# Dilated-attention transposes issued half a block later, MLP up products as one 512-column and one 256-column matmul

## The chip, the cores and the metric

One core of a Trainium2 chip runs the whole program. The metric is the device time of one launch in microseconds; the kernel before took 1325.72 us, the median of three runs (1324.39 to 1327.46).

## The reference, cut to what matters

Two transformer blocks run one after the other on 256 tokens of width 1024, in float32. The first block has four layers (Fourier mixing, grouped-query attention, dilated attention, Fourier mixing), each with a memory attention, a gate, an output projection and a layer norm. The second has two layers, each of three parallel mixers and a squared-ReLU MLP.

```
# first block, dilated layer (i = 2): three groups of 16 heads, rotated q and k, one softmax over the groups
for g, (window, dil) in enumerate(DIL_PAIRS):
    qg = apply_rope(qkv[:, :, 0, g], ang_1d)
    kg = apply_rope(qkv[:, :, 1, g], ang_1d)
    og, lg = dilated_group_attention(qg, kg, qkv[:, :, 2, g], dil, window // (2 * dil))
...
# second block, end of each of its two layers: h is 256 x 1024, w1 1024 x 4096, w2 4096 x 1024
jnp.square(jax.nn.relu(h @ w1)) @ w2
```

## The kernel before, in words

Every large product runs in three float32r matmuls: each operand is cut into a high part (a cast, on ScalarE) and a low part (the difference, on VectorE), and high by high, high by low and low by high are summed in one PSUM bank (class `Group`, `add`, line 221). The weights come in pieces of 128 x 1024 by DMA on SP's queue, are cut by `split_w` (lines 162 and 164) and used in the order of `plan()`. The activations are held transposed as `xTh` and `xTl`, [128, 8, 256] each: eight chunks of 128 features by 256 tokens. PSUM has eight banks, in four tags: `acc` (3), `sc` (2), `tp` (2), `pv` (1).

The framework puts each engine's instructions into one order, ahead of the run, by its own simulated timeline and by priority in program order; on the chip each engine then executes its list in that order. `tc.issue_after(ins)` forces instructions behind `ins` on its engine.

Dilated layer (`layer_dilated`): after one block for the memory queries, 18 blocks of 512 projected columns follow; `proj_N` computes a block in four steps of 12 matmuls (each step one weight piece for both halves of the tokens) into two `acc` banks, one for each half of 128 tokens. A block holds four 128-column kinds; a pair of heads has nine kinds (q and k of three groups, then three v), so that a q and its k can lie in two blocks. `rope` (line 714) rotates q and k: for each half, two VectorE products into the tiles `t1` and `t2` (lines 726, 727; two buffers each), and two GpSimd additions into `t1` (line 204). As soon as q and k of a group are both rotated, four TensorE transposes (line 899) put them into one `sc` bank, which is then cut into high and low. `weave` runs two steps of the blocks and then a step of each live pair of heads (`pair_dilated`: scores at line 238 into two `sc` banks, softmax at line 835 and after, transposes at line 537, values at lines 850 and 857). A pair becomes ready when its last v has been cut.

Between the dilated layer and the last Fourier layer the normed rows of x are transposed by `transpose_x` (line 306) with order "seq": four transposes into one `sc` bank, and then four casts and four differences of 128 x 128, each of which reads the bank in permuted column order (lines 193, 194). With the other orders it is one cast and one difference of 128 x 512.

MLP (end of `layer2`): 4096 hidden columns in eight blocks of 512. `up0` computes the first block; `up(b)` the seven others with `proj_T`: for each of four weight pieces, four chunks of 128 hidden columns and two chunks of features, three matmuls with 256 moving columns (the tokens), two chunks in one bank of two `tp` banks. A bank is then evacuated by a ReLU on ScalarE, a product on VectorE, a cast and a difference. `down(n, hf)` multiplies a hidden chunk by its row of w2, six matmuls of 512 columns for each half, into four banks (two `acc`, two `sc`) that stay open over the whole MLP. The order is up(b+1), then the eight calls of down for block b.

Of the kernel before, what the change touches and what calls it, by code (L numbers as in the profile page):

```python
# [17 lines left out]
P = 128  # L18
# [58 lines left out]
def kernel(ctx: ExitStack, tc: tile.TileContext, x_in, wall, vec, tabs, small, out, dbg=None):  # L77
# [113 lines left out]
    def split(h, l, src, scale=None, eng=None):  # L191
        if scale is None:
            A.copy(out=h, in_=src)  # L193
            return (eng or V).tensor_tensor(out=l, in0=src, in1=h.bitcast(F32), op=ALU.subtract).ins  # L194
        else:
            A.activation(out=h, in_=src, func=AF.Copy, scale=scale)
            return (eng or V).scalar_tensor_tensor(
                out=l, in0=src, scalar=scale, in1=h.bitcast(F32), op0=ALU.mult, op1=ALU.subtract).ins
# [49 lines left out]
    def hl(pair, f):  # L248
        return f(pair[0]), f(pair[1])
# [26 lines left out]
    mhalf = cst.tile([P, 12], F32, name="mhalf")  # L276
    G.memset(mhalf, -0.5)
    x = cst.tile([P, 2, D], F32, name="x")
    xTh = cst.tile([P, 8, T], F32R, name="xTh")
    xTl = cst.tile([P, 8, T], F32R, name="xTl")  # L280
    for n in range(4):
        load_raw(n)
    nc.sync.dma_start(x[:, 0, :], x_in[0:P, :])
# [17 lines left out]
    def transpose_x(hf, blk, src, order_):  # L301


        tp = scp([P, 4, P])
        for j in range(4):
            PE.transpose(tp[:, j, :], src[:, j * P:(j + 1) * P], ident)
        k = slice(4 * blk, 4 * blk + 4)
        if order_ == "seq":
            for j in range(4):
                f = lambda t: t[:, 4 * blk + j, hf * P:(hf + 1) * P].rearrange("p (a b c) -> p a b c", a=8, b=4, c=4)  # L310
                r = split(f(xTh), f(xTl), tp[:, j, :].rearrange("p (c b a) -> p a b c", a=8, b=4, c=4))
        else:
            c = slice(hf, T, 2) if order_ == "class" else slice(hf * P, (hf + 1) * P)
            r = split(xTh[:, k, c], xTl[:, k, c], tp)
        sc_read.append(r)

    def mm_out(dst, key, ys, npieces, by_class=False, ready=lambda i: True, n_end=0):
# [399 lines left out]

    def rope(ps, n, cos, sin, w, eng=None):

        t1 = ab.tile([P, 512], F32, tag="t1", name="t1", bufs=2)  # L720
        t2 = ab.tile([P, 512], F32, tag="t2", name="t2", bufs=2)
        v = lambda t: t[:, :n * 64].rearrange("p (n d) -> p n d", d=64)
        b = lambda t: t.unsqueeze(1).to_broadcast([P, n, 64])
        src = ps.rearrange("p (n d) -> p n d", d=64)
        with tc.high_priority():
            V.tensor_tensor(out=v(t1), in0=src, in1=b(cos), op=ALU.mult)
            V.tensor_tensor(out=v(t2), in0=src, in1=b(sin), op=ALU.mult)  # L727
        four = lambda t: t[:, :n * 64].rearrange("p (n t w) -> p n t w", t=2, w=w)
        for s in range(2):
            pool_add(four(t1)[:, :, s, :], four(t1)[:, :, s, :], four(t2)[:, :, 1 - s, :])  # L730
        return t1
# [130 lines left out]
    def layer_dilated(i):  # L862
        key = "c"
        kinds = []
        for p in range(8):
            kinds += [(p, "q", 0), (p, "k", 0), (p, "q", 1), (p, "k", 1), (p, "q", 2), (p, "k", 2)]
            kinds += [(p, "v", 0), (p, "v", 1), (p, "v", 2)]
        roped, vt, qm = {}, {}, []

        def projections(b):  # L870
            ps = yield from proj_N(key, 1 + b)
            cur = kinds[4 * b:4 * b + 4]
            s = 0
            while s < 4:
                e = s
                while e < 4 and (cur[e][1] == "v") == (cur[s][1] == "v") and cur[e][0] == cur[s][0]:
                    e += 1
                for hf in range(2):
                    src = ps[hf][:, s * P:e * P]
                    if cur[s][1] != "v":  # L880
                        r = rope(src, 2 * (e - s), rtab[:, hf, 2, :], rtab[:, hf, 3, :], 32)
                        for n in range(s, e):
                            roped[cur[n], hf] = r[:, (n - s) * P:(n - s + 1) * P]
                    else:
                        for n in range(s, e):
                            if cur[n] not in vt:
                                vt[cur[n]] = ph([P, 2, 2, P])
                            t = vt[cur[n]]
                            with tc.high_priority():
                                split(t[:, 0, hf, :], t[:, 1, hf, :], ps[hf][:, n * P:(n + 1) * P])  # L890
                s = e
            for p in range(8):
                for g in range(3):
                    kk = [(p, "q", g), (p, "k", g)]
                    if all((a, 0) in roped for a in kk):
                        tp = scp([P, 2, T])
                        for s, a in enumerate(kk):
                            for hf in range(2):
                                PE.transpose(tp[:, s, hf * P:(hf + 1) * P], roped.pop((a, hf)), ident)
                        t = (ph([P, 2, T]), ph([P, 2, T]))  # L900
                        sc_read.append(split(t[0], t[1], tp))
                        vt[p, "qk", g] = t

        def fill():
            qm.append((yield from tail(key, 0, True)))
            for b in range(18):
                yield from projections(b)
            yield from gates(key, 19)
            yield from out_and_norm(i, ORDER[2], "seq")

        def ready(c):
            return bool(qm) if c >= 8 else (c, "v", 2) in vt

        def pair(c):
            if c >= 8:
                return memory_pair(qm[0], c - 8)
            return pair_dilated([vt.pop((c, "qk", g)) for g in range(3)], [vt.pop((c, "v", g)) for g in range(3)], c)

        weave(fill(), [(lambda c=c: ready(c), lambda c=c: pair(c)) for c in ORDER[2]], 2, 3)

        for hf in range(2):
            for c in range(4):
                nc.gpsimd.dma_start(
                    scratch[hf * P:(hf + 1) * P, :].rearrange("(a b c) d -> c b a d", a=8, b=4, c=4)[c],
                    x[32 * c:32 * c + 32, hf, :])
        for hf in range(2):
            nc.gpsimd.dma_start(x[:, hf, :], scratch[hf * P:(hf + 1) * P, :])
# [88 lines left out]
    def layer2(l):  # L1016
# [371 lines left out]
                hid[k] = (hs[k // 2 * 2][:, k % 2, :], hs[k // 2 * 2 + 1][:, k % 2, :])  # L1388

        def up(b):  # L1390
            ps = run(proj_T(f"m1{l}", b, alloc=tpp))
            for j in range(2):
                s = pt([P, 2, T])
                A.activation(out=s, in_=ps[j], func=AF.Relu)
                V.tensor_tensor(out=s, in0=s, in1=ps[j], op=ALU.mult)
                h_, l_ = ph2([P, 2, T]), ph2([P, 2, T])
                split(h_, l_, s)
                for k in range(2):
                    hid[4 * b + 2 * j + k] = (h_[:, k, :], l_[:, k, :])
# [212 lines left out]
```

## Time and profile before

| what | value |
|---|---|
| median of three runs | 1325.72 us |
| time of the profiled execution | 1325.35 us |
| its span | 1323.6 us |
| TensorE busy | 1268.0 us (96%), 7550 matmuls |
| VectorE busy | 961.0 us (73%) |
| ScalarE busy | 750.6 us (57%) |
| GpSimd busy | 179.7 us (14%) |
| HBM traffic | 156 GB/s over the span |

The span is the time from the first to the last instruction of the profiled execution; its own time is 1.75 us longer. A busy share is an average over stages, and matmuls are pipelined: the duration of one is longer than the distance from its start to the start of the next, so what one costs is read from the starts.

### The profile page before, as it was taken

The page shows a single profiled execution, that of the slowest core. Times are in us where ns is not written, and L with a number is a line of the kernel's source. Part 1 is how long each engine was busy: PE and PEld are TensorE (multiplying, and loading weights), DVE is VectorE, ACT ScalarE, POOL GpSimd, SP SyncE. Part 2 cuts the span into 40 slices and gives each one's busy share as a digit, 9 for nine tenths or more (in the row PEclk, how much of TensorE's full clock was granted, in tenths as well). Part 3 has the DMA queues.
Part 4 walks back from the last instruction along what each step waited for, and adds up shares of the span by engine and source line. Part 5 has one row for each costly group of instructions (what it writes and reads, how often), then busy time and mean ns, then how long its engine had stood idle before and what let it go on. Part 6 is the DMA issues. An engine that isn't in the chain of part 4 may idle for free. (4 is left out here: it accounts for less than half of the span.)

```text
span 1323.6 us, 21769 instructions
## 1 busy us (share of the span) xinstructions
PE 1268.0 (96%) x7550; PEld 1090.7 (82%) x7550; DVE 961.0 (73%) x1950; ACT 750.6 (57%) x1673; POOL 179.7 (14%) x290
## 2 busy tenths in 40 slices
PE   8999998899999999998998999999999999999997
PEld 6987896688778878897986897899897897789896
DVE  7788887788778767777777896755556886665654
ACT  5664676555555645663653785545454774554543
POOL 1131500111112111122132201000001201000000
PEclk9999999999999999999998999999999999999999
DMA  8564542264334534355564543565664443366651
GB/s 289 175 221 144 163 148 80 92 194 158 108 121 153 158 115 128 128 169 174 177 198 138 184 138 110 178 205 181 186 187 151 145 154 127 132 218 185 184 189 49
DMA packets 64062, 209.53 MB, mean 158 GB/s; under 512 B 8520, under 2 KB 10192, under 8 KB 63952
## 3 DMA queue, kind: packets, MB, share of 16 engines
q1 hardware_dynamic: 60480, 203.33, 47.9%
q0 software_dynamic: 1888, 3.15, 0.8%
q10 hardware_dynamic: 1584, 1.67, 0.4%
q8 instruction: 59, 0.97, 0.3%
q14 instruction: 51, 0.42, 0.1%
HBM read 204.97 MB, written 2.10 MB: 156 GB/s over the span
## 5 line engine op out<-in xcount | busy, mean ns | idle before, releaser
L164 DVE TENSOR_TENSOR wl<-raw,wh 128x512 fp32r<-128x512 f32 (+3 forms) x756 | 502.7, 690 | 201.1 <-ACT wh L162 195.6
L162 ACT CAST wh<-raw 128x512 fp32r<-128x512 f32 (+3 forms) x756 | 441.8, 608 | 299.4 <-issue 74.7
L221 PE MATMUL acc<-wh,ph 128*128 128x512 f32 (+2 forms) x672 | 224.1, 389 | 6.3 <-ACT ph L548 2.0
L221 PE MATMUL acc<-wh,xTh 128*128 128x512 f32 (+3 forms) x560 | 218.7, 392 | 3.6 <-ACT xTh L193 2.2
L221 PE MATMUL acc<-wl,xTh 128*128 128x512 f32 (+3 forms) x560 | 216.9, 388 | 3.6 <-DVE wl L164 3.6
L221 PE MATMUL acc<-wh,xTl 128*128 128x512 f32 (+3 forms) x560 | 216.0, 388 | 2.5 <-DVE xTl L194 2.5
L221 PEld LDWEIGHTS acc<-wh,ph 128*128 128x128 f32 x672 | 125.1, 189 | 36.5 <-ACT ph L193 4.6
L221 PE MATMUL acc<-wl,ph 128*128 128x512 f32 (+2 forms) x336 | 130.3, 388 | 0.0
L221 PE MATMUL tp<-xTl,wh 128*128 128x256 f32 x448 | 126.6, 283 | 0.0
L221 PE MATMUL tp<-xTh,wl 128*128 128x256 f32 x448 | 126.6, 283 | 0.0
L221 PE MATMUL tp<-xTh,wh 128*128 128x256 f32 x448 | 126.6, 283 | 0.0
L221 PEld LDWEIGHTS acc<-wh,xTh 128*128 128x128 f32 x560 | 107.1, 191 | 23.5 <-ACT xTh L193 4.1
L221 PEld LDWEIGHTS acc<-wh,xTl 128*128 128x128 f32 x560 | 106.8, 191 | 23.1 <-DVE xTl L194 5.1
L221 PEld LDWEIGHTS acc<-wl,xTh 128*128 128x128 f32 x560 | 107.1, 191 | 21.6 <-DVE wl L164 4.3
L221 PE MATMUL sc<-wh,ph 128*128 128x512 f32 (+1 forms) x328 | 104.2, 369 | 0.0
L221 PE MATMUL acc<-xTh,wh 128*128 128x256 f32 x336 | 96.2, 287 | 0.0
L221 PE MATMUL acc<-xTh,wl 128*128 128x256 f32 x336 | 96.0, 286 | 0.0
L221 PE MATMUL acc<-xTl,wh 128*128 128x256 f32 x336 | 95.6, 285 | 0.0
L204 POOL TENSOR_TENSOR t<-t,t 128x256 f32<-128x256 f32 (+3 forms) x84 | 54.1, 673 | 268.4 <-DVE t L727 238.7
L221 PEld LDWEIGHTS tp<-xTl,wh 128*128 128x128 f32 x448 | 85.6, 191 | 0.5
L221 PEld LDWEIGHTS tp<-xTh,wh 128*128 128x128 f32 x448 | 85.5, 191 | 0.6
L221 PEld LDWEIGHTS tp<-xTh,wl 128*128 128x128 f32 x448 | 85.7, 191 | 0.0
(263 smaller groups left out, 2105.9 us busy)
## 6 DMA issues: line engine op xcount, KB each, us to landing
raw<-in_wall_dram SPq DMA_DIRECT2D x338, 512.0 KB, 3.9
raw<-in_wall_dram SPq DMA_DIRECT2D x20, 384.0 KB, 3.7
ph<-in_vec_dram SPq DMA_DIRECT2D x20, 256.0 KB, 6.0
raw<-in_wall_dram SPq DMA_DIRECT2D x8, 422.0 KB, 4.0
gn<-in_vec_dram SPq DMA_DIRECT2D x5, 512.0 KB, 4.7
raw<-in_wall_dram SPq DMA_DIRECT2D x6, 288.0 KB, 3.1
raw<-in_wall_dram SPq DMA_DIRECT2D x6, 256.0 KB, 3.9
x<-in_x_in_dram SPq DMA_DIRECT2D x2, 512.0 KB, 8.0
```

What stands on the lines that cost most here:

```text
L162: ih = A.copy(out=h[:, :k], in_=t[:, c]).ins
L164: il = V.tensor_tensor(out=l[:, :k], in0=t[:, c], in1=h[:, :k].bitcast(F32), op=ALU.subtract).ins
L204: G.tensor_tensor(out=out, in0=a, in1=b, op=ALU.add)
L221: done[0] = PE.matmul(out=self.out, lhsT=s, rhs=m, start=(i == 1), stop=(i == bk["n"]), skip_group_check=True).ins
```

## The change

Four edits:

1. `xTh` and `xTl` become the two halves of one tile `xT` [128, 8, 2, 256], so that a feature chunk's high and low part lie side by side.
2. For order "seq" the transposes write the permuted column order into PSUM, and one cast and one difference of 128 x 512 follow, as with the other orders.
3. In the dilated layer the transposes of a rotated group are not issued at the end of its block: the group is put on the list `waiting`, and `flush` issues the transposes after two of the four steps of the next block, behind the last matmul of a `Group`. After the last block it is called once more. The rotated tiles move from the tag `t1` (2 buffers) to a tag `rot` of 4 buffers, and a pair is ready when its three rotated groups are there as well as its last v.
4. `up(b)` multiplies the high weights by high and low activations in one matmul of 512 columns and the low weights by the high activations in one of 256, each chunk in a bank of its own (two `tp`, one `pv`, one `acc`). The evacuation copies the second half of the bank (ScalarE), adds the first (VectorE), and computes the squared ReLU in one VectorE instruction.

```diff
-    xTh = cst.tile([P, 8, T], F32R, name="xTh")
-    xTl = cst.tile([P, 8, T], F32R, name="xTl")
+    xT = cst.tile([P, 8, 2, T], F32R, name="xT")
+    xTh, xTl = xT[:, :, 0, :], xT[:, :, 1, :]
...
         for j in range(4):
-            PE.transpose(tp[:, j, :], src[:, j * P:(j + 1) * P], ident)
+            to = tp[:, j, :].rearrange("p (a b c) -> p c b a", a=8, b=4, c=4) if order_ == "seq" else tp[:, j, :]
+            PE.transpose(to, src[:, j * P:(j + 1) * P], ident)
         k = slice(4 * blk, 4 * blk + 4)
-        if order_ == "seq":
-            for j in range(4):
-                f = lambda t: t[:, 4 * blk + j, hf * P:(hf + 1) * P].rearrange("p (a b c) -> p a b c", a=8, b=4, c=4)
-                r = split(f(xTh), f(xTl), tp[:, j, :].rearrange("p (c b a) -> p a b c", a=8, b=4, c=4))
-        else:
-            c = slice(hf, T, 2) if order_ == "class" else slice(hf * P, (hf + 1) * P)
-            r = split(xTh[:, k, c], xTl[:, k, c], tp)
+        c = slice(hf, T, 2) if order_ == "class" else slice(hf * P, (hf + 1) * P)
+        r = split(xTh[:, k, c], xTl[:, k, c], tp)
...
-        t1 = ab.tile([P, 512], F32, tag="t1", name="t1", bufs=2)
+        t1 = pool1.tile([P, 512], F32, tag="rot", name="rot", bufs=4)
...
+        def flush():
+            with tc.issue_after(done[0]):
+                for p, g, rs in waiting:
+                    tp = scp([P, 2, T])
+                    for n, r in enumerate(rs):
+                        PE.transpose(tp[:, n // 2, (n % 2) * P:(n % 2 + 1) * P], r, ident)
+                    t = (ph([P, 2, T]), ph([P, 2, T]))
+                    sc_read.append(split(t[0], t[1], tp))
+                    vt[p, "qk", g] = t
+            waiting.clear()
+        def behind_half(steps):
...
+                n += 1
+                if n == 2:
+                    flush()
+                yield
         def projections(b):
-            ps = yield from proj_N(key, 1 + b)
+            ps = yield from behind_half(proj_N(key, 1 + b))
...
-                        tp = scp([P, 2, T])
-                        for s, a in enumerate(kk):
-                            for hf in range(2):
-                                PE.transpose(tp[:, s, hf * P:(hf + 1) * P], roped.pop((a, hf)), ident)
-                        t = (ph([P, 2, T]), ph([P, 2, T]))
-                        sc_read.append(split(t[0], t[1], tp))
-                        vt[p, "qk", g] = t
+                        waiting.append((p, g, [roped.pop((a, hf)) for a in kk for hf in range(2)]))
...
             for b in range(18):
                 yield from projections(b)
+            flush()
...
-            return bool(qm) if c >= 8 else (c, "v", 2) in vt
+            return bool(qm) if c >= 8 else all((c, *k) in vt for k in (("qk", 0), ("qk", 1), ("qk", 2), ("v", 2)))
...
         def up(b):
-            ps = run(proj_T(f"m1{l}", b, alloc=tpp))
+            ps = [f([P, 2, T]) for f in (tpp, tpp, pvp, acc)]
+            for i in range(4):
+                w = W(f"m1{l}", 4 * b + i)
+                for c in range(4):
+                    for kk in range(2):
+                        k = 2 * i + kk
+                        h_, l_ = hl(w, lambda t: t[:, kk * 512 + c * P:kk * 512 + (c + 1) * P])
+                        PE.matmul(out=ps[c], lhsT=h_, rhs=xT[:, k, :, :], start=(k == 0), stop=False, skip_group_check=True)
+                        done[0] = PE.matmul(out=ps[c][:, 0, :], lhsT=l_, rhs=xTh[:, k, :], start=False, stop=(k == 7),
+                                            skip_group_check=True).ins
             for j in range(2):
-                s = pt([P, 2, T])
-                A.activation(out=s, in_=ps[j], func=AF.Relu)
-                V.tensor_tensor(out=s, in0=s, in1=ps[j], op=ALU.mult)
+                r, s = pt([P, 2, T]), pt([P, 2, T])
+                for k in range(2):
+                    A.copy(out=r[:, k, :], in_=ps[2 * j + k][:, 1, :])
+                    V.tensor_tensor(out=s[:, k, :], in0=ps[2 * j + k][:, 0, :], in1=r[:, k, :], op=ALU.add)
+                V.scalar_tensor_tensor(out=s, in0=s, scalar=0.0, in1=s, op0=ALU.max, op1=ALU.mult)
                 h_, l_ = ph2([P, 2, T]), ph2([P, 2, T])
                 split(h_, l_, s)
```

## Rows read from the trace of the kernel before

**Rows 1.** The page's busy shares (busy us, share of the span, instructions).

```profile
PE 1268.0 (96%) x7550; PEld 1090.7 (82%) x7550; DVE 961.0 (73%) x1950; ACT 750.6 (57%) x1673; POOL 179.7 (14%) x290
```

**Rows 2.** Waits of TensorE: line, releaser, us in total, times, longest us.

```profile
PE sc L899 <- POOL t L204: 4.8, 2, 2.4
PE acc L221 <- DVE wl L164: 3.8, 3, 3.4
```

**Rows 3.** Chain that ended last, second MLP: start us, us, engine, tile, line, count.

```profile
1149.09 11.50 PE tp L221 x96
...
1163.86 1.40 PE acc L221 x6
```

**Rows 4.** Timeline of TensorE, dilated layer: start us, us, instruction, count [idle before].

```profile
337.20 0.44 PE L899 MATMUL sc<-ident,t 128*128 128x128 f32 x2 [0.21 <-DVE st L835]
340.02 0.74 PE L899 MATMUL sc<-ident,t 128*128 128x128 f32 x2 [2.38 <-POOL t L204]
340.51 0.79 PE L221 MATMUL acc<-wh,xTh 128*128 128x512 f32 x1
...
342.38 0.63 PE L221 MATMUL acc<-wl,xTh 128*128 128x512 f32 x1
342.81 0.63 PE L221 MATMUL acc<-wh,xTl 128*128 128x512 f32 x1
```

**Rows 5.** Timeline of VectorE and of GpSimd in the same stretch.

```profile
337.63 0.56 DVE L726 TENSOR_TENSOR t<-acc,rtab 128x384 f32<-128x384 f32 x1 [0.49 <-PE sc L899]
...
338.83 2.47 POOL L204 TENSOR_TENSOR t<-t,t 128x192 f32<-128x192 f32 x4 [16.81 <-DVE t L727]
```

**Rows 6.** Stretches: from:to, length, busy us (instructions) by engine, granted clock, DMA.

```profile
340.50:343.70 3.20, 3.20 (x9) 2.52 (x9) 1.88 (x5) 1.39 (x4) 0.80 (x2) 0.50 0.02 5
...
479.90:483.60 3.70, 3.70 (x10) 2.90 (x10) 2.23 (x6) 1.85 (x4) 0.81 (x2) 0.56 0.02 4
```

**Rows 7.** Timeline of VectorE and GpSimd, 512-column rotation of a later block.

```profile
361.02 0.69 DVE L726 TENSOR_TENSOR t<-acc,rtab 128x512 f32<-128x512 f32 x1 [0.18 <-PE sc L899]
...
366.28 2.18 POOL L204 TENSOR_TENSOR t<-t,t 128x256 f32<-128x256 f32 x2 [1.92 <-DVE t L727]
```

**Rows 8.** Timeline of TensorE, 512-column matmuls of `up0`.

```profile
839.82 0.39 PE L221 MATMUL acc<-wh,xTl 128*128 128x512 f32 x1
...
841.19 0.39 PE L221 MATMUL acc<-wh,xTl 128*128 128x512 f32 x1
```

**Rows 9.** Groups by form: count, busy us, mean ns, idle before and releaser.

```profile
L1395 DVE TENSOR_TENSOR pt<-pt,tp 128x512 f32<-128x512 f32 x28 | 19.1, 684 | 7.6 <-ACT pt L1394 7.6
L693 DVE TENSOR_TENSOR sg<-sc,pt 128x256 f32<-128x256 f32 x8 | 3.4, 419 | 1.5 <-ACT pt L692 1.5
L377 DVE SCALAR_TENSOR_TENSOR pt<-x,st,gn 128x512 f32<-128x512 f32 x16 | 11.3, 746 | 7.0 <-POOL st L369 7.0
```

**Rows 10.** Stretch of the first MLP, columns as in rows 6.

```profile
850.00:1004.00 154.00, 154.00 (x971) 138.80 (x970) 91.13 (x140) 80.38 (x140) 0.00 (x0) 1.00 0.60 186
```

**Rows 11.** Groups by form: the cuts behind the transposes of x.

```profile
L193 ACT CAST xTh<-sc 128x512 fp32r<-128x512 f32 x28 | 16.2, 591 | 23.9 <-PE sc L306 23.6
L194 DVE TENSOR_TENSOR xTl<-sc,xTh 128x512 fp32r<-128x512 f32 x28 | 18.8, 681 | 1.5 <-ACT xTh L193 1.5
L194 DVE TENSOR_TENSOR xTl<-sc,xTh 128x128 fp32r<-128x128 f32 x16 | 4.3, 283 | 2.7 <-ACT xTh L193 2.7
L193 ACT CAST xTh<-sc 128x128 fp32r<-128x128 f32 x16 | 4.0, 266 | 9.7 <-DVE xTl L194 5.3 <-PE sc L306 4.4
```

**Rows 12.** Timeline of VectorE before the last Fourier layer.

```profile
618.27 1.40 DVE L433 SCALAR_TENSOR_TENSOR x<-x,st,ph 128x512 f32<-128x512 f32 x2
619.59 1.28 DVE L164 TENSOR_TENSOR wl<-raw,wh 128x512 fp32r<-128x512 f32 x2
```

**Rows 13.** Line 306 there: count, ns min/median/max, first and last start.

```profile
L306 PE MATMUL sc<-ident,x x12: 271/273/421, 612.3 to 622.8; 128*128 128x128 f32 x12
```

More of the change, by code (lines that the diff above doesn't have):

```diff
@@ L868, in layer_dilated @@
         roped, vt, qm = {}, {}, []
+        waiting = []
+        def flush():
[9 more added lines that the diff above has]
+        def behind_half(steps):
+            n = 0
+            while True:
+                try:
+                    next(steps)
+                except StopIteration as e:
+                    return e.value
+                n += 1
+                if n == 2:
+                    flush()
+                yield
         def projections(b):
-            ps = yield from proj_N(key, 1 + b)
+            ps = yield from behind_half(proj_N(key, 1 + b))
             cur = kinds[4 * b:4 * b + 4]
```

## The prediction

> **What bounds the kernel now.** I read the page's busy shares first. TensorE is busy for 1268.0 of 1323.6 us (96%), VectorE for 73% [rows 1]: little time is to be had by feeding TensorE better, and the rest only by giving it less to do. So two questions follow: where do the 55 us without TensorE lie, and which matmuls cost more than their columns?
>
> For the first I read what TensorE waited for. Two of its longer waits lie where the change works: the transposes of line 899 waited for GpSimd twice, 2.4 us each time, and one wait for the low part of a weight piece, before the last Fourier layer, took 3.4 us [rows 2].
>
> For the second I read the chain that ended last through an MLP. It is TensorE alone: 96 matmuls of `up` in 11.50 us, then groups of six `down` matmuls of 1.40 us each, without a hole [rows 3]. In the whole stretch of 154 us TensorE is busy for 154.00 us at the full granted clock (1.00, the level of 2.4 GHz) [rows 10]. There every nanosecond off the distance between matmuls is a nanosecond off the span.
>
> **The dilated layer (edit 3).** The timeline of TensorE shows how a wait of 2.4 us arises [rows 4]. At 337.20 two transposes run, 2.82 us later two more, and only then do the projections go on. VectorE's rotation begins at 337.63, released by the first two transposes (its releaser is line 899), and GpSimd's additions run from 338.83 to 341.30 and release the other two [rows 5]. By the code this is a q whose k lies in the next block: it keeps both `t1` buffers, so k's rotation can't be written until q has been transposed, and in TensorE's fixed order k's transposes stand right behind q's. TensorE must sit through a rotation.
>
> What it costs: 0.21 us before the first two and 2.38 us before the others [rows 4], 2.6 us together. Behind it the clock has fallen: from 340.50 to 343.70 it was granted at 0.50, which is the level of 1.2 GHz, and successive 512-column matmuls start 0.43 us apart (342.38, 342.81) [rows 4, 6]. A stretch of 3.20 us at 0.50 loses 1.6 us. At the second place 3.70 us at 0.56 loses 3.70 x 0.44 = 1.6 us as well [rows 6], and its wait is the other one of the two [rows 2]. So 4.2 us at each place, 8.4 us for both.
>
> Edit 3 takes away both conditions. With four buffers a q can wait for its k while the next block's rotation is written, and the transposes are put behind two of the four steps of the next block, 24 matmuls. At 0.228 us (below) these alone are 5.5 us in which the rotation can run; the one in rows 5 took 341.30 - 337.63 = 3.7 us. The number of transposes, cuts, DMAs and scores stays the same. What is queued behind a waiting transpose is everything on TensorE; the DMAs of SP's queue follow the weight cuts, which continue. What is late next: the two `acc` banks of a block come free when its rotation has read them, now without the wait for `t1`, and the pair whose last k and last v share a block (2 of 8 pairs) starts half a block later, beside projections that fill TensorE anyway. For the last pair the extra `flush` stands where the transposes stood. I take -8.4 us. Bounds: at best the whole distance between the two pairs of transposes goes with the slow clock, 2 x (2.82 + 0.21 + 1.6) = 9.3 us; at worst TensorE waits in the new places as long as in the old ones, 0, or longer (the slower rival below).
>
> **MLP up (edit 4).** An `up` is 32 pairs of weight chunk and feature chunk, three matmuls of 256 columns each, 11.50/96 = 119.8 ns apart [rows 3]. Afterwards each pair is one matmul of 512 and one of 256 columns: the same 768 columns, one matmul (and one weight load) less, 448 in the 14 calls. At 2.4 GHz 256 columns last 106.7 ns and 512 last 213.3 ns, so a 256-column matmul costs 13.1 ns above its columns. For 512 columns two rows bound the price. In `up0`, where the same activations and weights are multiplied, six matmuls take 841.19 - 839.82 = 1.37 us, 228 ns each [rows 8], 15 ns above the columns. In `down` it is 1.40/6 = 233 ns [rows 3], 20 ns above. I take 228 ns, since its operands are those of `up`, only with the roles exchanged. Then an `up` is 32 x (228 + 119.8) = 11.13 us, 0.37 us less, and 14 of them give -5.2 us. With 233 ns it is 0.21 us each, -2.9 us. The ends: -6.0 us (448 x 13.4 ns) if the surplus stays at 13.1 ns, and 0 if a 512-column matmul costs as much as two of 256; a loss would need more than 240 ns at the full clock, above both rows.
>
> The Trainium skill, "TensorE: Matmul & The Clock Gate", section "Back-to-back issue gap", gives the isolated distance of matmuls as columns/2.4 plus 2.5 ns. By that rule the matmul saved would be worth about 2.5 ns, an estimate of 448 x 2.5 ns = 1.1 us, and the forecast would be some 4 us later; the 119.8 ns of rows 3 against its 109 ns speak against it.
>
> The evacuation gets dearer beside this. Per call VectorE has four additions of 256 columns and two squares of 512 instead of two products: 4 x 419 + 2 x 746 - 2 x 684 = 1.8 us more [rows 9]. In the stretch of rows 10, which holds about seven calls, VectorE is idle for 63 us, 9 us for each, and ScalarE for 74 us. The cover is the eight groups of `down` for the block before, 8 x 1.40 = 11.2 us [rows 3], by whose end both the hidden chunks and the four banks must be ready. I cost it at nothing; without that cover it is 1.8 x 14 = 25 us.
>
> **Order "seq" (edits 1 and 2).** Four calls had 4 x (266 + 283) = 2.2 us of cuts in alternation on ScalarE and VectorE, and get 591 + 681 = 1.3 us [rows 11], 0.9 us less each. But the hole before the last Fourier layer ends with the low part of a weight piece, which starts at 619.59 behind the norm's last product (618.27, two of them) [rows 12]; the cuts stand beside that. Against it the 16 transposes now write PSUM with steps. No row shows such a write; the slowest transpose in this place lasted 421 ns against a median of 273 [rows 13], so I bound the cost by 16 x 148 ns = 2.4 us; the eight for the first half of the tokens run before the hole and are hidden in it, which leaves 1.2 us. Between -1.8 us (the two calls for the second half of the tokens, were they on the path) and +1.2 us I take 0, since a chain untouched by it ends the hole. The joint tile `xT` changes only addresses: 0.
>
> The Trainium skill, "PSUM — Partial Sum Buffer", section "Specifications (TRN2)", says that a non-contiguous access pattern slows matmuls significantly. By that rule edit 2 would cost something near the upper end, and the sum would be 1313 us; no run here shows it yet.
>
> **The sum.** 1325.35 (the profiled execution) - 8.4 - 5.2 + 0 = 1311.75 us. The median of the runs stands 0.37 us above that execution, so 1312.1: I predict 1312 us. Its own range is 1309 (-9.3 - 6.0 - 1.8) to 1320 (half the dilated gain, -2.9 and +1.2).
>
> **The rivals.**
> - The waits of the dilated layer move instead of going: the new transposes stand in TensorE's fixed order too, and a rotation late by two microseconds stops them again. For it: the order comes from a simulated timeline, and it was wrong in the two old places. Against it: in 16 of 18 blocks it wasn't. Only the MLP gains: 1325.7 - 5.2 = 1320.5 us. Chance 0.18.
> - The surplus of a matmul grows with its columns, so that 512 costs nearly two of 256. For it: 20 ns in `down` against 13.1. Against it: 15 ns in `up0`. MLP gain 1 us: 1325.7 - 8.4 - 1 = 1316 us. Chance 0.11. The Trainium skill's rule on the distance ("TensorE: Matmul & The Clock Gate", "Back-to-back issue gap") would end here too.
> - Neither edit does what it says: the waits move and the 512-column matmul is dear. 1325.7 - 1 = about 1325 us. Chance 0.07.
> - Slower: in the wide blocks (512 rotated columns, 6 of 18) the rotation is later than the half block. One row shows it: VectorE began at 361.02, and GpSimd ended at 366.28 + 2.18 = 368.46, 7.4 us, with weight cuts between [rows 7], against 5.5 us for 24 matmuls. If TensorE sat for the 1.9 us each time and lost 1.6 us to the clock, six blocks would cost 21 us: 1312 + 21 = 1333 us. It decides from four such blocks on. Against it: TensorE also has the pairs' scores and values between, and VectorE has high priority for the rotation. Chance 0.08.
>
> The forecast itself has 0.56.
>
> **How the numbers follow.** About 0.2%, 2.7 us, is what a measurement here can tell from no change. The forecast and the first two rivals are faster by more than that: 0.85. The third is the same: 0.07. The fourth is slower: 0.08. For 8 in 10 the range reaches from 1306 (the best ends, and 2 to 3 us for pauses that I haven't counted) up to 1321, which takes in the first two rivals.
>
> **What would show it.** Right: no wait of line 899 for GpSimd near 2.4 us, and the clock at 1.00 through the dilated layer; 32 matmuls of 512 columns and 32 of 256 in about 11.1 us for each `up`; 7102 matmuls in all. Wrong: a wait of the transposes in `flush` followed by a stretch at 0.50; an `up` of 11.3 us or more; TensorE idle between `down` and the next `up` for a bank or a hidden chunk.

## The result, and the profile after

The changed kernel takes 1316.66 us (median of 4 runs, 1315.59 to 1317.85) against 1326.59 us for the kernel before on the same chip: ratio 0.9927, 95% interval 0.9909 to 0.9945, 9.9 us less. The profiled execution took 1315.77 us, its span 1314.1 us. So the change is faster by more than the 0.2% that can be told here, and inside the range, but 4.7 us short of the 1312 us forecast (3.8 us, if the gain of 9.9 us is set beside the 13.7 us that the forecast took off its own median before).

The page's busy shares of the kernel after answer to [rows 1]:

```profile
PE 1260.3 (96%) x7102; PEld 1063.0 (81%) x7102; DVE 979.2 (75%) x1994; ACT 751.4 (57%) x1689; POOL 187.1 (14%) x290
```

The 7102 matmuls are the number that the prediction named. TensorE is busy for 7.7 us less, the span is 9.5 us shorter, and VectorE has 18 us more to do.

To see where the time went I cut both traces at the first transposes of x of each stage. Each number is the distance between two such starts, in us; the last stage ends with the last matmul:

```
                    before    after   difference
start, first layers 259.49   260.31     +0.82
dilated layer       352.80   348.33     -4.47
Fourier layer        94.51    93.72     -0.79
mixers, first       121.01   121.54     +0.53
MLP, first          185.55   183.46     -2.09
mixers, second      117.78   116.24     -1.54
MLP, second         185.74   183.62     -2.12
```

The dilated layer gained half of the 8.4 us forecast, the two MLPs 4.2 of 5.2 us. These are the stages of one execution each; the other four, where the forecast had nothing, sum to 1.0 us less.

**The dilated layer.** What TensorE waited for there, in the kernel after (line, releaser, us in total, times, longest us; it answers to the first row of [rows 2]):

```profile
PE pv L847 <- ACT PTh L193: 3.0, 5, 0.8
PE tp L534 <- DVE PTl L194: 1.2, 3, 0.4
PE acc L221 <- DVE xT L194: 0.9, 1, 0.9
PE tp L534 <- DVE pt L836: 0.7, 1, 0.7
```

The two waits of 2.4 us for GpSimd are gone, as forecast: the rotated transposes (now line 875) wait for nobody. In their place the values (`pv`, line 847) wait five times for the cut of the transposed softmax. In the kernel before this wait is there too, but twice, 1.5 us together:

```profile
PE pv L850 <- ACT PTh L193: 1.5, 2, 0.7
```

TensorE's timeline after shows one such place (start us, us, instruction, count [idle before]):

```profile
349.25 0.60 PE L875 MATMUL sc<-ident,rot 128*128 128x128 f32 x4
349.68 0.60 PE L534 MATMUL tp<-ident,pt 128*128 128x128 f32 x4
351.01 0.49 PE L847 MATMUL pv<-PTh,ph 128*128 128x512 f32 x1 [0.73 <-ACT PTh L193]
351.85 0.65 PE L534 MATMUL tp<-ident,pt 128*128 128x128 f32 x4 [0.34 <-DVE PTl L194]
352.26 0.48 PE L847 MATMUL pv<-PTl,ph 128*128 128x512 f32 x1
```

The reader sees the old fault in a new place: a transpose (line 534), and right behind it, in TensorE's fixed order, the product that needs its result. ScalarE's cast and VectorE's subtraction must run in between, and nothing else stands there for TensorE. To price this I charged each matmul the distance from its start to the next start and summed over the stage, before and after. The 96 rotated transposes cost 5.6 us less and the 512-column matmuls of line 221 (projections above all) 3.0 us less: 8.6 us, the forecast. The first values (lines 850 and 847) cost 2.2 us more and the softmax transposes 1.9 us more: 4.1 us given back.

**The MLP.** The chain that ended last, in an `up` of the second MLP (start us, us, engine, tile, line); in [rows 3] such a product was one row, 96 matmuls in 11.50 us; now groups of `down` stand between its parts:

```profile
1145.99 0.23 PE tp L1417
1146.22 0.12 PE tp L1418
1146.34 0.24 PE tp L1417
1146.58 0.12 PE tp L1418
...
1148.82 1.40 PE acc L221 x6
1150.22 1.40 PE sc L221 x6
```

Start to start, the 448 matmuls of 512 columns are 233.6 ns apart on average and the 448 of 256 columns 117.1 ns. An `up` is therefore 32 x 350.7 ns = 11.22 us, 0.28 us less than 11.50; the forecast had 0.37. The groups of six `down` matmuls still take 1.40 us, and TensorE has no hole (start, length, busy us (instructions) of PE, PEld, DVE, ACT, POOL, granted clock; [rows 10] before):

```profile
844.00:998.00 154.00, 154.00 (x768) 129.08 (x767) 100.32 (x170) 82.77 (x156) 0.00 (x0) 1.00 0.65 190
```

VectorE's 100.32 us (91.13 before) are the dearer evacuation. It stands beside TensorE, which has no hole.

### The profile page after: what moved, and what is told of

It reads as the page before. It is cut to its first block, busy times and chain, and to the rows that moved or that the text cites. A ratio compares the mean times of both kernels' runs of the same rounds, so it can differ in the third digit from the quotient of the medians.

```text
span 1314.1 us, 20879 instructions
## 1 busy us (share of the span) xinstructions
PE 1260.3 (96%) x7102; PEld 1063.0 (81%) x7102; DVE 979.2 (75%) x1994; ACT 751.4 (57%) x1689; POOL 187.1 (14%) x290
## 5 line engine op out<-in xcount | busy, mean ns | idle before, releaser
L221 PE MATMUL acc<-wh,xT 128*128 128x512 f32 (+3 forms) x1120 | 350.8, 388 | 5.8 <-DVE xT L194 2.5
L221 PEld LDWEIGHTS acc<-wh,xT 128*128 128x128 f32 x1120 | 206.8, 189 | 45.9 <-DVE xT L194 5.1
L221 PE MATMUL acc<-wl,xT 128*128 128x512 f32 (+3 forms) x560 | 214.6, 384 | 0.2 <-DVE wl L164 0.2
L221 PE MATMUL acc<-xT,wh 128*128 128x256 f32 x672 | 127.9, 286 | 0.0
L221 PEld LDWEIGHTS acc<-wl,xT 128*128 128x128 f32 x560 | 106.1, 190 | 17.6 <-DVE wl L164 0.5
L221 PEld LDWEIGHTS acc<-xT,wh 128*128 128x128 f32 x672 | 105.9, 191 | 1.4
L221 PE MATMUL acc<-xT,wl 128*128 128x256 f32 x336 | 95.6, 285 | 0.0
L1417 PE MATMUL tp<-xT,wh 128*128 128x512 f32 x224 | 80.9, 395 | 0.0
L221 PEld LDWEIGHTS acc<-wl,ph 128*128 128x128 f32 x336 | 63.8, 190 | 11.5
L221 PEld LDWEIGHTS acc<-xT,wl 128*128 128x128 f32 x336 | 64.1, 191 | 0.5
```

What stands on the lines that cost most here:

```text
L221: done[0] = PE.matmul(out=self.out, lhsT=s, rhs=m, start=(i == 1), stop=(i == bk["n"]), skip_group_check=True).ins
L1417: PE.matmul(out=ps[c], lhsT=h_, rhs=xT[:, k, :, :], start=(k == 0), stop=False, skip_group_check=True)
```

## The experiments

Each ratio is to runs of the kernel before on the same chip. On the chips used the kernel before has medians from 1323.6 to 1327.5 us, so two experiments compare best by their ratios; a stage is always that of one execution. "The planner" is the framework that makes each engine's order. The theory that they test: edit 3 does remove 8.6 us, but its order puts the values behind their transposes and gives 4.1 us back. The rivals: the give-back comes from other edits; the buffers alone would have done it; the waits belong to holding back as such.

**The MLP edit alone.** The diff is edit 4 as shown above, with the joined `xT`, on the kernel before.

> The kernel before with the MLP up products alone changed (edit 4; the joined xT tile goes with it). By the trace of after, an up product's 64 matmuls start 233.6 ns (512 columns) and 117.2 ns (256) apart, 32 x (233.6 + 117.2) = 11.23 us against 11.50, so 14 x 0.27 = 3.8 us. Theory: the MLP's gain stands alone: 3.8 us (3.0 to 4.6) less than the kernel before, ratio 0.9971, and nothing changes ahead of the first mixer. Rival: the joined xT tile changes the planner's order elsewhere, and part of the 4.1 us of new waits in the dilated layer belongs to this edit: then 0 to 2 us less only, and the values in the dilated layer stand directly behind their transposes at more than two places.

1321.55 us, ratio 0.997 (0.996 to 0.998). Its two MLPs take 183.49 and 183.63 us, as in the whole change, and its dilated layer 352.34 (352.80 before). The edit stands alone; 3.8 us was expected, and 4.5 measured by the medians, 4.0 by the ratio. Of its trace's gain 1.5 us again lie in the second mixers (below).

**The sequence-order transposes alone.**

```
+            to = tp[:, j, :].rearrange("p (a b c) -> p c b a", a=8, b=4, c=4) if order_ == "seq" else tp[:, j, :]
+            PE.transpose(to, src[:, j * P:(j + 1) * P], ident)
```

> The kernel before with the last transposes of the dilated layer written in sequence order (edit 2 alone), one evacuation where there were four. Theory of the prediction: nothing on the path, -1.0 to +0.5 us; the traces of the whole change put 0.8 us less there, from the layer's end to the first mixer. Rival, by the Trainium skill, PSUM — Partial Sum Buffer, section on the TRN2 specifications: the scattered write of PSUM slows these transposes; if each of the eight took twice its 109 ns, the kernel would be up to 0.9 us slower.

1325.86 us, ratio 1.0001 (0.999 to 1.0011): nothing, as forecast.

**Four rotation buffers alone.** One line on the kernel before; no transpose is held back:

```
-        t1 = ab.tile([P, 512], F32, tag="t1", name="t1", bufs=2)
+        t1 = pool1.tile([P, 512], F32, tag="rot", name="rot", bufs=4)
```

> The kernel before with nothing but four buffers in place of two for the first rotation product (renamed rot). Theory: the rotated transposes waited because they stood directly behind their rotation, not for a buffer: no difference, -0.5 to +0.5 us, and TensorE's wait for the rotation (two places of about 2.6 us in the two narrow blocks) is still there. Rival: the second pair of buffers alone lets VectorE and GpSimd run the rotation ahead: then most of 8.4 us goes without moving a transpose, and moving them is what added the 4.1 us of new waits, so this kernel would be 4 to 8 us faster than before.

1318.88 us, ratio 0.995 (0.9936 to 0.9963): 7.2 us less by the medians, 6.6 by the ratio. My theory fell here and the rival stood. The waits for GpSimd are gone without a moved line. (The line also moves the tile to another pool; no run keeps two buffers there.) TensorE's timeline at the place of [rows 4]:

```profile
340.00 1.29 PE L238 MATMUL sc<-ph 64*128 64x128 f32 x18
341.21 0.66 PE L537 MATMUL tp<-ident,pt 128*128 128x128 f32 x4
341.63 0.48 PE L221 MATMUL acc<-wh,xTh 128*128 128x512 f32 x1
...
346.30 0.39 PE L221 MATMUL acc<-wh,xTl 128*128 128x512 f32 x1
346.53 0.60 PE L899 MATMUL sc<-ident,rot 128*128 128x128 f32 x4
```

With two buffers the transposes stood behind the softmax transposes, two of them waiting; with four, the planner itself puts 21 projection matmuls ahead, and the four stand together and wait for nothing. The waits left in the layer:

```profile
PE pv L850 <- ACT PTh L193: 1.8, 4, 0.6
PE acc L221 <- DVE xTl L194: 0.9, 1, 0.9
PE tp L221 <- ACT xTh L193: 0.8, 2, 0.6
PE tp L537 <- DVE PTl L194: 0.6, 2, 0.4
```

Here too the values wait oftener than before, four times for two: the new order alone brings some of it. The layer takes 345.30 us.

**The dilated part alone** (edit 3, buffers included).

> The kernel before with the dilated layer's part alone (edit 3 with its four buffers). Theory: it takes off 8.4 us of waits and slow clock at the rotated transposes and gives 4.1 us back, since the planner now puts the values directly behind the softmax transposes at five places instead of two: 4.4 us less than before (3.5 to 5.5), ratio 0.9967. Rival: the new waits come from the other edits by way of the planner's order: then 7.5 to 8.5 us less, ratio 0.994, and the trace has the values behind the transposes at two places as before. With the runs of the MLP edit alone and the sequence edit alone the sum should meet the whole change's 9.7 us if the parts do not act on each other.

1322.2 us, ratio 0.9979 (0.9966 to 0.9992): 3.9 us less by the medians, but 2.8 by the ratio, where 4.4 (3.5 to 5.5) was expected; and 3.3 us (3.8 by the ratios) more than the buffers alone, whose interval it does not meet. Its waits:

```profile
PE pv L850 <- ACT PTh L193: 3.0, 5, 0.8
PE tp L537 <- DVE PTl L194: 1.2, 3, 0.4
```

They are those of the whole change, so they come with edit 3 and not with the others. The three parts alone give 0.9979 x 1.0001 x 0.997 = 0.995, the whole change 0.9927: 3 us apart, which the intervals just allow. The traces show where executions can differ by as much: this one has a stretch of low clock in the layer and one in the second mixers, that of the whole change neither (below).

**The whole change without the held-back transposes:** buffers, edits 1, 2 and 4.

> The whole change without its moved transposes: four rotation buffers, the sequence-order transposes and the MLP up products, while the rotated transposes stand where they stood before. Theory, after the run with the four buffers alone (7.2 us less than before, against 3.9 for the whole dilated part): the second pair of buffers is what ends TensorE's wait for the rotation; holding the transposes back a block only adds waits of the values. Then the parts sum: 7.2 + 4.5 + 0.2, so 1314.1 us beside a before of 1326 (ratio 0.991), some 2 to 3 us under the whole change. Rival: the buffers' gain and the other edits do not add (the planner orders anew), and this is at the whole change's 1316.7 or above.

1313.48 us, ratio 0.9906 (0.9889 to 0.9924). The dilated layer takes 345.32 us, 3.0 us less than after, with four waits of the values:

```profile
PE pv L846 <- ACT PTh L193: 1.8, 4, 0.6
```

The parts add within the interval (0.995, 1.0001 and 0.997 give 0.992). By time alone the interval still meets that of the change; the stage tells them apart.

**Three buffers in that kernel** (`bufs=3`).

> As the run before it, but three rotation buffers in place of four. If a buffer per rotated tile of a group of four were needed, three would keep part of the wait at the rotated transposes (2.4 us at a place) and this is 2 to 7 us slower than with four. If the two buffers only forced the planner to issue the transposes early, three set them free as well; the order built with three has the values directly behind the softmax transposes at three places instead of four, so it would be 0 to 1.5 us faster than with four.

1314.72 us, ratio 0.9913 (0.9896 to 0.993), 1.2 us above four buffers, which neither expectation names and the intervals do not separate. The trace does:

```profile
PE tp L533 <- DVE pt L835: 2.5, 1, 2.5
PE sc L895 <- DVE st L831: 1.6, 1, 1.6
...
PE sc L895 <- POOL rot L204: 0.7, 1, 0.7
```

With three the rotated transposes (line 895) wait again at one place, 1.6 and 0.7 us, and the softmax transposes 2.5 us at another; the layer takes 348.22 us. (Its profiled execution, 1317.35 us, is the slowest of five, so the stage may be on the long side.)

**Held back to the third quarter.** On the kernel after:

```
-                if n == 2:
+                if n == 3:
                     flush()
```

> The kernel after, with the held-back transposes issued behind the third quarter of the next block's projections in place of the second. In the order built from it the values stand directly behind the softmax transposes in one pair of heads, in the kernel after in five; nothing else of the change is touched. Theory (the 4.1 us of new waits come from that order): the waits at four of the five places go, 0.8 to 1.5 us each with the slow clock behind them, and the kernel is 3 to 5 us faster than after: 1312 to 1314 us. Rival: the waits belong to holding the transposes back at all (pairs start a block later, and something else is late then): the same time as after, 1316 to 1317, with the waits elsewhere.

1311.34 us, ratio 0.9891 (0.9873 to 0.9908): 4.8 us less by the ratios (0.9927 - 0.9891 = 0.0036 of 1326), and the layer takes 343.14 us, 5.2 us less. One place is left:

```profile
PE pv L847 <- ACT PTh L193: 0.8, 1, 0.8
PE tp L534 <- DVE PTl L194: 0.4, 1, 0.4
```

So holding back is not what costs; the order that came of it is. The two intervals (after: 0.9909 to 0.9945) only just do not meet.

**Held back to the first quarter** (`n == 1`).

> The kernel after with the held-back transposes issued behind the first quarter of the next block in place of the second. The order built from it has the values directly behind the softmax transposes in three pairs of heads (five in after, one with the third quarter). Theory: the time goes by the number of such places, so it lies between: 1313 to 1315 us, if the rotation is already done there; the transposes then stand 5.5 us behind their block instead of 11. Rival: an earlier place is a worse one (GpSimd's share of the rotation ends after the first quarter), TensorE waits for the rotation again, some 2 us at a place, and it is 1317 us or above.

1313.11 us, ratio 0.9897 (0.9879 to 0.9914), which can't be told from after or from the third quarter; the layer takes 345.03 us, and the values wait at three places:

```profile
PE pv L847 <- ACT PTh L193: 1.7, 3, 0.8
...
PE tp L534 <- DVE PTl L194: 0.4, 1, 0.4
```

**Third quarter, and three steps of fill to one of the pairs.**

```
-        weave(fill(), [(lambda c=c: ready(c), lambda c=c: pair(c)) for c in ORDER[2]], 2, 3)
+        weave(fill(), [(lambda c=c: ready(c), lambda c=c: pair(c)) for c in ORDER[2]], 3, 3)
```

> The held-back transposes behind the third quarter, and the fill of the dilated layer woven three steps to one of the pairs, where there were two. In the order built from it no pair of heads has its values directly behind its softmax transposes (one in the run with the third quarter alone, five in the kernel after): before each first product of values stand at least 3072 columns of other work. Theory: the last such place goes too, 0.8 + 0.6 us, so 1 to 2 us under the run with the third quarter alone: 1310 us. Rival: the pairs' last steps fall behind the end of the projections with three steps to one, and the layer's end, where the x transposes and the 3.3 us hole before the Fourier layer stand, is late: 1312 to 1318 us.

1308.38 us, ratio 0.9864 (0.9848 to 0.988): faster than both kernels, with intervals apart from both. No wait of the values is left:

```profile
PE acc L221 <- DVE xT L194: 0.9, 1, 0.9
PE tp L221 <- DVE xT L194: 0.2, 1, 0.2
PE sc L308 <- DVE x L430: 0.2, 1, 0.2
```

Four kernels now differ only in where the held-back transposes and the pairs' steps fall:

```
places where values wait   0        1        3        5
dilated layer, us          341.53   343.14   345.03   348.33
```

That is 6.8 us for five places, 1.36 us each on average; from column to column it is 1.61, 0.95 and 1.65 us a place. The waits themselves are 0, 1.2, 2.1 and 4.9 us. The rest is overlap lost: at 351.01 in the timeline above TensorE is idle for 0.73 us, but the start before lies 1.00 us back. The 4.1 us given back would be three places at that average. The price does not carry over to another order: the two kernels with four buffers, the old weave and nothing held back have four places and take 345.3 us, 0.9 us a place above the 341.53.

**No holding back, four steps of fill to one.** The kernel of the fifth experiment with `4, 3` in the weave.

> No transposes held back: four rotation buffers, the sequence-order transposes, the MLP up products (1313.5 us with the weave as before), and the dilated layer's fill woven four steps to one of the pairs instead of two. In the order built from it no pair of heads has its values directly behind its softmax transposes: at least 3072 columns of other work stand between. Theory: what counts are the rotation buffers and the distance between the softmax transposes and their values; holding the rotated transposes back a block is not needed for either. Then the waits of the values are gone as in the run with the third quarter and three steps to one: 1308 to 1310 us. Rival: without holding back, TensorE waits for the rotation once the pairs move (or the layer's end comes late, with four steps to one): 1311 us or above.

1313.07 us, ratio 0.992 (0.9901 to 0.994): the rival's time, and by the reason in its bracket. Up to 590 us TensorE is fed; then the last pairs stand alone (columns as in the stretch above):

```profile
262.00:590.00 328.00, 327.53 (x1893) 275.59 (x1894) 256.51 (x534) 186.70 (x404) 59.24 (x84) 1.00 0.50 151
590.00:601.00 11.00, 8.63 (x37) 6.39 (x36) 4.12 (x7) 1.83 (x4) 0.74 (x1) 0.84 0.01 1
596.00:600.50 4.50, 3.77 (x10) 2.98 (x10) 1.64 (x4) 0.40 (x1) 0.74 (x1) 0.62 0.01 4
```

In the second row 2.4 of 11 us are idle, and after them the clock is granted at 0.62. Up to 590 us TensorE is idle for 0.5 of 328 us, so in the body of the layer the buffers and the distance do without holding back. In the whole layer nothing is won (346.86 us; 345.32 with two steps to one). Whether a weave with a better end would reach 1308 us without holding back is not shown.

**The 512-column up matmul split again.** On the kernel after, same banks, same evacuation:

```
-  PE.matmul(out=ps[c], lhsT=h_, rhs=xT[:, k, :, :], start=(k == 0), stop=False, skip_group_check=True)
+  PE.matmul(out=ps[c][:, 0, :], lhsT=h_, rhs=xTh[:, k, :], start=(k == 0), stop=False, skip_group_check=True)
+  PE.matmul(out=ps[c][:, 1, :], lhsT=h_, rhs=xTl[:, k, :], start=False, stop=False, skip_group_check=True)
```

> The kernel after with each 512-column up matmul of the MLP split again into two of 256 columns, into the same banks; the four banks, the evacuation by ScalarE and VectorE and the joined xT tile stay as in the change. Theory (the gain is the time per matmul: two of 256 columns start 2 x 119.8 ns apart in sum in the kernel before, the one of 512 takes 233.6): 448 of them by 2 x 119.8 - 233.6 = 6.0 ns is 2.7 us, and 672 instead of 448... the 256-column ones at 117.2 to 119.8 ns, so 1.5 to 3.9 us slower than after. Rival: the banks and the evacuation were what gained (the up products no longer share a bank in turn), and the split one is within 0.5 us of after.

1321.22 us, ratio 0.9966 (0.9954 to 0.9978). The MLPs take 185.54 and 185.67 us, where the kernel before has 185.55 and 185.74: the whole gain is undone, and the new evacuation and banks are worth neither a gain nor a loss. The gain is the matmul saved. By the ratios it is 5.2 us above after (0.0039 of 1326), more than the 1.5 to 3.9 us expected. The two MLPs are 4.1 us longer; in this trace the second mixers too are 1.5 us longer, 117.79 us here and 116.24 in after, and the dilated layer 1.4 us, though this edit touches neither (below).

**Two of 512, then two of 256 columns.**

> The kernel after with the up products' matmuls written two of 512 columns, then two of 256, in place of turn by turn. Theory of the mis-sized term: the surplus of the 512-column matmul (233.6 ns here, 228 in the first up product read before) belongs to the turn between the two shapes; with half the turns 224 of 448 pairs would cost 228 + 119.8 and not 350.8 ns, so 0.7 us less than after, too little for a verdict but to be read in the spacing of the starts. Rival: the surplus belongs to the operands (weights stationary, x moving, a bank per chunk) and not to the turns: the spacing of the starts stays at 233 to 234 ns for 512 columns, and the time at 1316.7 us.

1315.27 us, ratio 0.9914 (0.9899 to 0.9928), too near to tell from after. The spacing answers: 512 columns 233.3 ns, so turning less often does not bring it to 228, and the rival holds; 256 columns 115.5 ns instead of 117.1, and both MLPs are 0.4 us shorter (183.06, 183.21). That the operands are the cause is not shown either: in `up0` of the kernel before, with the same operands, six matmuls from 838.67 us are 230 ns apart and six from 840.05 us 227 ns. Why 512 columns cost 233 ns here stays open.

## Why the prediction was right or wrong

**What bounds the kernel: right.** In the MLPs the distances between the starts give 4.1 us less (below), and the stages are 4.2 us shorter; in the dilated layer the waits that went are in the stage, and so are those that came.

**The number: partly luck.** 1316.66 us is what the second rival gave (1316), but not by its mechanism: the MLPs gained 4.2 us and not 1, and the dilated layer 4.5 and not 8.4.

**The dilated layer: the removed part was right, the sum wrong.** The two waits and their slow clock went, 8.6 us for a forecast of 8.4; no transposes in `flush` wait; the stretch of the layer (262 to 608 us) is granted 1.00. The step that failed is "what is late next": I wrote that the pair which starts half a block later stands "beside projections that fill TensorE anyway". But TensorE's order is fixed, and the planner made it anew. Softmax transposes and values moved against the projections, and at five places instead of two too little stands between them: +4.1 us. Not all of that comes from holding back: with the buffers alone there are four places, and the layer is 345.30 us, 1.1 us above the 344.2 that 352.80 - 8.6 leaves. I had read the waits of values at the two old places as no part of the change. The first rival (the waits move) was thus half right, at another instruction than it named.

The prediction also said that the edit takes away both conditions. One was enough: with four buffers the transposes leave their place without being held back. My reading of why they waited (q keeps both `t1` buffers) fits that run, and it should have told me that.

**MLP up: mechanism right, one term too large.** I took 228 ns for 512 columns and it is 233.6; the other end that I gave, 233 ns, was right. The 256-column one is cheaper than taken, 117.1 for 119.8 ns. Over all 1344 matmuls of `up` before, the distance is 120.0 and not 119.8 ns, so the gain is 448 x (359.9 - 350.7) = 4.1 us; the two stages show 4.2. An `up` of 11.22 us lies between my sign of being right (11.1) and that of being wrong (11.3). The saved matmul is worth 350.7 against 359.8 ns (the split kernel), 9 ns of 120. The Trainium skill, "TensorE: Matmul & The Clock Gate", section "Back-to-back issue gap", would put it at 2.5 ns by its formula for isolated matmuls; here it is 9, and the measurement decides. The cover of the evacuation held: the split kernel, with the new evacuation, has the MLPs of the kernel before.

**Order "seq": right at 0.** Alone it is 1.0001. The Trainium skill, "PSUM — Partial Sum Buffer", section "Specifications (TRN2)", says that non-contiguous access slows matmuls significantly. The transposes here do not show it: those that write with steps start 108 to 109 ns apart, as do those of line 875 (349.25, above) and those of the kernel before, without steps. In the timeline after:

```profile
608.64 0.60 PE L308 MATMUL sc<-ident,x 128*128 128x128 f32 x4
...
616.24 1.94 PE L308 MATMUL sc<-ident,x 128*128 128x128 f32 x8 [3.10 <-DVE x L430]
```

The eight at 616.24 are slow because the clock is at 0.50 there, after the hole of 3.1 us (columns as above):

```profile
616.20:618.40 2.20, 2.16 (x9) 2.10 (x10) 2.20 (x4) 0.77 (x2) 1.58 (x4) 0.50 0.46 168
```

They start 213 ns apart, as the plain ones at 622.20 us in the kernel before, at the same clock. The hole itself is about as long as before (3.35 us), but ends with x's norm instead of a weight's low part.

**The slower rival** (the rotation late in six wide blocks) did not come: not one wait of line 875 for GpSimd.

**What was in no term.** The second mixers, whose code no edit touches, are 1.5 us shorter after. In the kernel before, the clock is low in one stretch there:

```profile
1101.60:1105.20 3.60, 3.60 (x12) 2.89 (x11) 0.28 (x1) 0.02 (x1) 0.16 (x1) 0.53 0.02 5
```

In the kernel after, work from the same place of the stage is granted 1.00:

```profile
1095.60:1099.20 3.60, 3.60 (x19) 2.96 (x18) 0.91 (x3) 1.18 (x3) 0.19 (x1) 1.00 0.00 0
```

A stretch of 3.6 us at 0.53 loses 1.7 us. It is there in seven of the fourteen traces (117.6 to 117.8 us) and not in the others (116.2 to 116.3). All five traces whose `up` has three 256-column matmuls have it (before, the sequence order alone, the buffers alone, the dilated part alone, the split kernel), but only two of the nine with the 512-column one (three buffers, the first quarter). So edit 4, which changes when the mixers start, may help it to go, or it is chance; with one trace of each kernel neither is shown. A stage of one execution may differ by it.

## What to carry to other kernels

When a step is moved in a fixed order, list every pair "write, then need" that moves with it, and ask what will stand between the two afterwards; here five waits of 0.4 to 0.8 us, three more than before, undid half of what the move gained. Where an instruction must stand early only because a buffer has to come free, try more buffers before moving the instruction; if it is moved as well, try several places (the third quarter was 4.8 us better than the second). A matmul's price is read at the same shape, and the same roles of operands, or kept as a range.

## What the runs showed of the hardware

A wait does not always cost clock. The wait of 2.38 us before [rows 4] was followed by 0.50 (the level of 1.2 GHz). In the kernel after, the place with 0.73 and 0.34 us of idle keeps 1.00, though TensorE is busy for only 2.63 of 3.70 us:

```profile
349.50:353.20 3.70, 2.63 (x18) 1.91 (x16) 3.02 (x7) 2.64 (x9) 0.00 (x0) 1.00 0.00 0
```

So does the next place, with 0.69 and 0.57 us of idle:

```profile
382.00:386.00 4.00, 2.74 (x27) 1.90 (x26) 3.57 (x9) 3.03 (x10) 0.00 (x0) 1.00 0.02 4
```

Yet the dilated part alone, with the same order and waits, falls to half clock behind the same 0.69 and 0.56 us; 2.70 us of that stretch:

```profile
384.70:387.40 2.70, 2.70 (x17) 2.28 (x16) 2.43 (x11) 1.51 (x5) 0.61 (x2) 0.50 0.03 6
```

They lose 1.35 us, most of the 1.5 us by which its layer (349.85 us) is longer than that of the whole change (348.33 us). Of the four traces with this order in the layer two have the low stretch (this one and the split kernel, 349.8 us) and two have not (after, and two of 512 then two of 256). Equal waits, then, were followed by either level.

The twelve executions of the dilated part alone differ in the clock too: one took 1319.22 us at a mean granted clock of 0.995, another 1326.87 us at 0.986.
